# A down projection by seven products: other accumulators, another order of the products, and the operand sums moved behind one of them

## The chip, the cores and the metric

The kernel runs on one core of a Trainium2 chip. The core has five engines, each with its own queue of instructions: TensorE (PE in the profile; its weight loads are PEld), VectorE (DVE), ScalarE (ACT), GpSimd (POOL) and SyncE (SP), which issues most of the transfers. The metric is the device time of one execution in microseconds. TensorE writes its products into PSUM, which the kernel uses as eight banks of 128 x 512 fp32; everything else lies in SBUF.

## The reference

Two token batches, one of 512 and one of 256 tokens with 1024 features each, run through the same trunk of two layers. A layer is a feed-forward half step, a token mixer, and another feed-forward half step, each on a normalised input and added to the stream x:

```
x = x + 0.5 * swiglu_ffn(rmsnorm(x), w1, w2)
x = x + mixer(rmsnorm(x))
x = x + 0.5 * swiglu_ffn(rmsnorm(x), w1, w2)

gate, up = split(x @ w1, 2)          # w1 is 1024 x 5632
swiglu   = (silu(gate) * up) @ w2    # w2 is 2816 x 1024
```

There are four feed-forward steps in all. The mixers (a gated linear recurrence in the first layer, windowed attention in the second) are not touched by the change.

## The kernel before

All 768 tokens are handled together, as two halves of 384 (three blocks of 128 tokens). Every fp32 operand of a product is split into a high part, rounded to fp32r, and a low part that holds the rest. ScalarE makes the high part (a cast, L199 for weights and L266 for activations), VectorE the low part by a subtraction (L200 and L267). A product is then three matmuls: high by high, high by low, low by high.

A feed-forward step has 22 hidden chunks of 128. The first two go through the plain product. The others are treated as 2 x 2 block products that need seven block products instead of eight (a Strassen-Winograd scheme). The names p1 to p7 are these products. The weight blocks are a11, a12, a21 and a22. The weight operands of the seven are a11 (p1), a12 (p2), sums that are formed in place as the products are staged (p3, p6, p5), a22 (p4) and, for p7, two small tiles s3 that a transfer with addition on the POOL queue fills (L141).

**Up projection** (`up_pair`, L431). A pair of calls makes four hidden tiles, for two chunks and two token halves, named b00, b01, b10 and b11. In one call the products come in the order p1, p7, p2, p5, p4, p6, p3, each of 12 matmuls with 384 columns (`product`, L416). The tile for the second half is the last: it needs p3, then an addition (L453), the silu on ScalarE (L454), a product (L455), and the split into high and low part (L266, L267).

**Operand sums** (`mix`, L348, called through `gather`, L512). Four hidden tiles give the left operands of the down projection: b00, b10 and b11 directly, and t1 to t4 as sums of them (L350, L351, L353, L354), each of which is split as well. `FACTOR` (L45) says which product uses which operand: p1 b00, p2 b10, p3 b11, p4 t4, p5 t1, p6 t2, p7 t3. A group holds two sets of tiles (`kp` 0 and 1), the two K halves of its products.

**Down projection** (`down_quad`, L458). After each two pairs comes a group of seven products; there are five groups in a step (g = 0 to 4), 20 in the kernel. A product has three token blocks with a PSUM bank each, and six matmuls of 512 columns per block (two K halves by three; L479), so a group has 126. Every product has its result added from PSUM to the stream x by VectorE (`add_x`, L501), with factor 0.5 or -0.5. Three products add to the banks of another (`chain`): p2 to those of p1, p4 to those of p5, p3 to those of p7. Such a product may begin a block only when VectorE has read that bank. x itself is kept in a changed basis during the five groups: at g = 0 (L464, L465) and after the last group (L494, L495) sums of its four quarters are taken.

**Order.** The source order gives the priority; the instruction order of each engine is fixed when the program is built, by a planner that works with its own estimates of durations. An instruction whose inputs the planner thinks ready can be issued ahead of earlier ones of the source.

**Weights.** `plan_ffn` (L378) lists what is to be loaded. `load_next` loads the raw blocks into four raw buffers (L151, and L185 for s3). `stage_next` runs the next step of the listed order, which splits one operand. `done` gives back the slots of a product that has been issued and lets `ahead` stage as much as fits eight slots. A down operand takes two slots, so four are staged at a time: when a group begins, the first four of the listed order. In the step of p1, a11 is replaced by a11 + a21 (L206) once it has been split, and in the step of p2 a12 by a12 + a11 (L210). p3 is the split of the a12 so made.

Of the kernel before, what the change touches and what calls it, by code (L numbers as in the profile page):

```python
# [35 lines left out]
HB = H // P  # L36
# [4 lines left out]
SLOTS = 21  # L41
RING = 1024
UP = ("p1", "p7", "p2", "p5", "p4", "p6", "p3")
DOWN = ("p1", "p2", "p5", "p4", "p7", "p6", "p3")
FACTOR = {"p1": "b00", "p2": "b10", "p3": "b11", "p4": "t4", "p5": "t1", "p6": "t2", "p7": "t3"}  # L45


class Trunk:
# [291 lines left out]
    def put(self, name, kp, src):  # L340
        t = self.ops[(name, kp)] = self.big([P, 2, 2, H], F32R)
        self.split(src, t[:, :, 0, :], t[:, :, 1, :])
# [5 lines left out]
    def mix(self, b11, b12, b21, b22, put):  # L348
        sub = self.nc.vector.tensor_sub
        sub(b22, b12, b22)  # L350
        sub(b12, b11, b12)  # L351
        put("t1", b12)
        sub(b11, b11, b22)  # L353
        sub(b21, b21, b11)  # L354
        put("t4", b21)
        put("t3", b22)
        put("t2", b11)

    def sums(self):
        for kp in range(2):  # L360
# [17 lines left out]
    def plan_ffn(self, tag, w1, w2):  # L378
        def up(i):
            gate, up = (w1[:, c * P : (c + 1) * P] for c in (i, NF + i))  # L380
            if i < PLAIN:
                self.plan((tag, i, 0), gate, (NC, P))
                self.plan((tag, i, 1), up, (NC, P))
            else:
                self.plan_quad((tag, i), (gate, up), (NC, P), UP)

        for g in range(GROUPS):
            for i in range(4 * g, 4 * g + 4):
                up(i)
            rows = w2[4 * g * P : (4 * g + 4) * P, :].rearrange("(a k p) c -> k p a c", p=P, k=2)  # L390
            srcs = [rows[k][:, :, c * 512 : (c + 1) * 512] for c in range(2) for k in range(2)]
            self.plan_quad((tag, "down", g), srcs, (2, 512), DOWN)
        for i in range(NF - 2, NF):
            up(i)
        for c in range(2):
            self.plan((tag, "last", c), w2[(NF - 2) * P :, c * 512 : (c + 1) * 512], (2, 512))
# [58 lines left out]
        self.last_dve = nc.vector.tensor_mul(w, v, w).ins  # L455
        yield w

    def down_quad(self, tag, g, hid):  # L458
        nc = self.nc
        cols = lambda b, c: self.x[b][:, c * 512 : (c + 1) * 512]  # L460
        if g == 0:
            for i in range(HB):
                x12, x21, x22 = cols(HB + i, 0), cols(i, 1), cols(HB + i, 1)
                nc.vector.tensor_add(x12, x12, x22)  # L464
                nc.vector.tensor_sub(x21, x21, x22)  # L465
        banks = {}
        for name in DOWN:
            wh, wl = self.take((tag, "down", g, name))
            chain = {"p2": "p1", "p4": "p5", "p3": "p7"}.get(name, name)
            for i in range(HB):  # L470
                if name == chain:
                    banks[(chain, i)] = self.ps()
                ps = banks[(chain, i)]
                sl = slice(i * P, (i + 1) * P)
                for kp in range(2):
                    h = hid[FACTOR[name]]
                    a, w = (h[:, kp, 0, sl], h[:, kp, 1, sl]), (wh[:, kp, :], wl[:, kp, :])
                    for q, (x, y) in enumerate(((0, 0), (0, 1), (1, 0))):
                        nc.tensor.matmul(  # L479
                            ps,  # L480
                            a[x],
                            w[y],
                            start=name == chain and kp == 0 and q == 0,
                            stop=kp == 1 and q == 2,
                            skip_group_check=True,
                        )
                x22 = cols(HB + i, 1)
                dst = {"p2": cols(i, 0), "p4": cols(i, 1), "p3": cols(HB + i, 0)}.get(name, x22)
                self.add_x(dst, ps, -0.5 if name in ("p1", "p5") else 0.5)
            self.done((tag, "down", g, name))  # L490
        if g == GROUPS - 1:
            for i in range(HB):
                x12, x21, x22 = cols(HB + i, 0), cols(i, 1), cols(HB + i, 1)
                nc.vector.tensor_sub(x12, x12, x22)  # L494
                nc.vector.tensor_add(x21, x21, x22)  # L495

    def add_x(self, x, ps, c):
# [5 lines left out]
    def ffn(self, tag, next_row):  # L503
        for g in range(GROUPS):
            hid = {}

            def put(name, src, kp):
                if name not in hid:
                    hid[name] = self.big([P, 2, 2, H], F32R)
                self.split(src, hid[name][:, kp, 0, :], hid[name][:, kp, 1, :])  # L510

            def gather(ts, kp):  # L512
                self.mix(ts[0], ts[1], ts[2], ts[3], lambda name, src: put(name, src, kp))

            if g == 0:
                ts = {}
                for half in range(2):
                    for j in range(PLAIN):
                        t = ts[2 * j + half] = self.up_plain(tag, j, half)
                        name = f"b{j}{half}"  # L520
                        if name != "b01":
                            put(name, t, 0)
                gather(ts, 0)
                self.run_later(len(self.deferred))
            for kp in range(2):
                if g == 0 and kp == 0:
                    continue
                ts = []
                for j in range(2):
                    for half, t in enumerate(self.up_pair(tag, 4 * g + 2 * kp + j)):  # L530
                        ts.append(t)
                        name = f"b{j}{half}"
                        if name != "b01":
                            put(name, t, kp)
                gather(ts, kp)
            self.down_quad(tag, g, hid)
        hids = []
        for j in range(NF - 2, NF):
            hid = self.big([P, 2, T], F32R)
            for half, t in enumerate(self.up_pair(tag, j)):  # L540
                self.split(t, *(hid[:, i, half * H : (half + 1) * H] for i in range(2)))
            hids.append(hid)
        if next_row is None:
            self.load_final()
        banks = {}

        def add(b, k, hid):
            sl = slice(b * P, (b + 1) * P)
            for c in range(2):
                wh, wl = self.take((tag, "last", c))  # L550
                if k == 0:
                    banks[(b, c)] = self.ps()
                w = wh[:, k, :], wl[:, k, :]
                self.mm3(banks[(b, c)], (hid[:, 0, sl], hid[:, 1, sl]), w, k == 0, k == 1)
                if b == NBLK - 1 and k:
                    self.done((tag, "last", c))

        for b in range(NBLK):
            for i, k in (((0, 0), (1, 0), (0, 1)), ((1, 1),))[b] if b < 2 else ((b, 0), (b, 1)):
                add(i, k, hids[k])  # L560
            for c in range(2):
                self.add_x(self.x[b][:, c * 512 : (c + 1) * 512], banks[(b, c)], 0.5)
            self.after_block(b, next_row)
            if b >= 4:
                self.run_later()
# [716 lines left out]
```

## Time and profile before

| what | value |
| --- | --- |
| three runs, median (lowest to highest) | 2849.59 us (2848.89 to 2852.01) |
| the profiled execution, its own time | 2852.12 us |
| its span, first to last instruction | 2850.3 us |
| granted TensorE clock | 0.998 |
| matmuls of the up products (L421) | 6720, busy 1172.8 us |
| matmuls of the down products (L479) | 2520, busy 586.8 us |
| evictions to x (L501) | 468, busy 305.5 us |

The page lists the instructions of a kind with their busy time, the mean duration of one, and the idle time of their engine just before them, with what ended it. A matmul's recorded duration is longer than the distance from its start to the next one's start, because they overlap; so stretches on TensorE are better measured from start to start. The timeline merges neighbouring instructions of one line into a row: start, length, engine, line, operation, the count behind an x, and in brackets the idle time before it. Rows of stretches give the length, then for each engine its busy time and count.

### The profile page before, as it was taken

Reading aid. Unit: us, or ns where it says so; the run is one execution under the profiler, and the core shown is the slowest. Engines: PE = TensorE matmul, PEld = TensorE weight load, DVE = VectorE, ACT = ScalarE, POOL = GpSimd, SP = SyncE. Lnnn points to the kernel's source line nnn. Section 1 sums busy time; section 2 is a strip of 40 time slices with the busy share of each in tenths; the row PEclk is TensorE's granted clock in tenths of the full one; section 3 lists DMA queues with packets and bytes.
Section 4 is the critical chain, followed back from the end, with each engine's and each line's share of the span. In section 5 each row is a group of like instructions: output and inputs, shape, how many; then the busy total and the mean of one; then the engine's idle time right before and its main releaser. Section 6 shows DMA issues by size and latency. Waiting matters only on the chain. (4 is left out here: it accounts for less than half of the span.)

```text
span 2850.3 us, 40558 instructions
## 1 busy us (share of the span) xinstructions
PE 2796.7 (98%) x15225; PEld 2554.2 (90%) x15225; DVE 2173.2 (76%) x3750; ACT 1318.9 (46%) x2454; POOL 355.1 (12%) x402
## 2 busy tenths in 40 slices
PE   8999999999999999999999999999999899999998
PEld 8899999889899889998998998999888789989997
DVE  7788787468577658878878887887848878788877
ACT  7344443434344336434444643444458755434443
POOL 1111111000000001111111111111002211111110
PEclk9999999999999999999999999999999999999999
DMA  6554454311111133555444355545422113555443
GB/s 165 127 125 122 116 134 121 115 44 39 44 39 38 60 97 86 132 127 122 123 119 114 84 134 127 122 121 124 126 71 75 37 51 90 135 126 125 117 121 96
DMA packets 330101, 291.37 MB, mean 102 GB/s; under 512 B 11608, under 2 KB 257840, under 8 KB 329904
## 3 DMA queue, kind: packets, MB, share of 16 engines
q1 hardware_dynamic: 294064, 212.43, 25.4%
q0 software_dynamic: 31680, 62.93, 12.6%
q10 hardware_dynamic: 4160, 13.42, 1.3%
q8 instruction: 119, 1.95, 0.3%
q14 instruction: 78, 0.64, 0.1%
HBM read 216.39 MB, written 9.44 MB: 79 GB/s over the span
## 5 line engine op out<-in xcount | busy, mean ns | idle before, releaser
L421 PE MATMUL ps<-big,w 128*128 128x384 f32 x6720 | 1172.8, 334 | 3.1 <-DVE tA L444 2.9
L421 PEld LDWEIGHTS ps<-big,w 128*128 128x128 f32 x6720 | 1165.4, 188 | 8.8 <-DVE tA L444 7.2
L199 ACT CAST w<-wr 128x512 fp32r<-128x512 f32 x600 | 416.1, 707 | 722.7 <-PE ps L421 321.0
L479 PE MATMUL ps<-w,big 128*128 128x512 f32 x2520 | 586.8, 391 | 17.4 <-DVE x L501 17.4
L479 PEld LDWEIGHTS ps<-w,big 128*128 128x128 f32 x2520 | 469.4, 188 | 129.7 <-DVE x L501 17.3
L200 DVE TENSOR_TENSOR w<-wr,w 128x512 fp32r<-128x512 f32 (+1 forms) x520 | 438.1, 853 | 95.7 <-ACT w L199 87.0
L501 DVE SCALAR_TENSOR_TENSOR x<-ps,x 128x512 f32<-128x512 f32 x468 | 305.5, 682 | 20.5 <-PE ps L479 10.2
L141 POOL DMA_DIRECT2D s<-wr x120 | 105.4, 878 | 1333.4 <-DMA wr<-in_ffn_w_dram 583.0
L261 PE MATMUL ps<-w,big 128*128 128x512 f32 x624 | 249.8, 400 | 0.2
L263 PE MATMUL ps<-w,big 128*128 128x512 f32 x624 | 245.2, 393 | 2.5 <-DVE big L330 1.3
L262 PE MATMUL ps<-w,big 128*128 128x512 f32 x624 | 244.4, 392 | 0.0
L266 ACT CAST big<-tA 128x384 fp32r<-128x384 f32 x296 | 148.0, 513 | 175.0 <-DVE tA L449 72.0
L261 PE MATMUL ps<-big,w 128*128 128x384 f32 (+2 forms) x640 | 220.8, 346 | 3.3 <-ACT big L266 2.0
L262 PE MATMUL ps<-big,w 128*128 128x384 f32 (+2 forms) x640 | 216.8, 339 | 0.7 <-DVE big L267 0.5
L263 PE MATMUL ps<-big,w 128*128 128x384 f32 (+2 forms) x640 | 215.7, 337 | 0.0
L167 DVE TENSOR_TENSOR w<-wr,w 128x1024 fp32r<-128x1024 f32 x92 | 111.6, 1222 | 83.6 <-ACT w L166 59.7
L141 POOL DMA_DIRECT2D wr<-wr x100 | 87.5, 875 | 680.0 <-DVE tA L350 319.8
L267 DVE TENSOR_TENSOR big<-tA,big 128x384 fp32r<-128x384 f32 x296 | 164.2, 566 | 7.9 <-ACT big L266 4.4
L206 DVE TENSOR_TENSOR wr<-wr,wr 128x512 f32<-128x512 f32 (+1 forms) x100 | 79.3, 793 | 114.5 <-DMA wr<-wr 85.9
L166 ACT CAST w<-wr 128x1024 fp32r<-128x1024 f32 x92 | 96.6, 1052 | 120.5 <-PE ps L262 99.7
L263 PEld LDWEIGHTS ps<-w,big 128*128 128x128 f32 x624 | 117.4, 188 | 28.8 <-DVE big L330 2.0
L261 PEld LDWEIGHTS ps<-w,big 128*128 128x128 f32 x624 | 117.8, 189 | 22.3 <-issue 0.6
(170 smaller groups left out, 3317.2 us busy)
## 6 DMA issues: line engine op xcount, KB each, us to landing
wr<-in_ffn_w_dram SPq DMA_DIRECT2D x264, 512.0 KB, 3.9
s<-in_ffn_w_dram SPq DMA_DIRECT2D x120, 256.0 KB, 3.0
s<-wr POOLq DMA_DIRECT2D x120, 256.0 KB, 4.0
wr<-wr POOLq DMA_DIRECT2D x80, 256.0 KB, 4.0
wr<-in_hg_w_in_dram SPq DMA_DIRECT2D x40, 512.0 KB, 3.8
wr<-wr POOLq DMA_DIRECT2D x20, 512.0 KB, 4.6
spill<-x ACTq DMA_DIRECT2D x12, 512.0 KB, 3.0
x<-spill ACTq DMA_DIRECT2D x12, 512.0 KB, 3.3
```

The costliest lines, as they stand in the source:

```text
L141: self.nc.gpsimd.dma_start(out, src, accum_op=ALU.add)
L167: self.nc.vector.tensor_sub(lo, raw, hi.bitcast(F32))
L199: nc.scalar.copy(h, src)
L200: (eng or nc.vector).tensor_sub(l, src, h.bitcast(F32))
L261: nc.tensor.matmul(out, a[0], b[0], start=first, stop=False)
L262: nc.tensor.matmul(out, a[0], b[1], start=False, stop=False)
L263: nc.tensor.matmul(out, a[1], b[0], start=False, stop=last)
L266: self.nc.scalar.copy(hi, src)
L267: self.nc.vector.tensor_sub(lo, src, hi.bitcast(F32))
L421: self.nc.tensor.matmul(ps, a[x], b[y], start=first and k == 0 and i == 0, stop=k == 3 and i == 2, skip_group_check=True,)
L479: nc.tensor.matmul(ps, a[x], w[y], start=name == chain and kp == 0 and q == 0, stop=kp == 1 and q == 2, skip_group_check=True,)
L501: self.nc.vector.scalar_tensor_tensor(x, ps, c, x, ALU.mult, ALU.add)
```

## The change

The list `DOWN` says in which order the products are issued; a second list, `DOWN_STAGED`, says in which order their weights are staged (before, one list served both). The accumulators change: p2 still adds to p1's banks and p4 to p5's, p7 now adds to p3's. The results go to other quarters of x with other signs, and the basis at the first and after the last group is changed to fit. The number of matmuls and evictions stays.

The operand sums of the second set (`gather(ts, 1)`) are no longer formed before the group begins in the source, but inside it, ahead of p2, that is behind p1, p3 and their evictions. Within `mix` each sum is split as soon as it exists: t3, t1, t2, t4.

```diff
-DOWN = ("p1", "p2", "p5", "p4", "p7", "p6", "p3")
+DOWN = ("p1", "p3", "p2", "p7", "p5", "p6", "p4")
+DOWN_STAGED = ("p1", "p2", "p3", "p7", "p5", "p6", "p4")
...
         sub(b22, b12, b22)
         sub(b12, b11, b12)
+        put("t3", b22)
         put("t1", b12)
         sub(b11, b11, b22)
+        put("t2", b11)
         sub(b21, b21, b11)
         put("t4", b21)
-        put("t3", b22)
-        put("t2", b11)
...
-            self.plan_quad((tag, "down", g), srcs, (2, 512), DOWN)
+            self.plan_quad((tag, "down", g), srcs, (2, 512), DOWN_STAGED)
...
-    def down_quad(self, tag, g, hid):
+    def down_quad(self, tag, g, hid, gather):
...
                 x12, x21, x22 = cols(HB + i, 0), cols(i, 1), cols(HB + i, 1)
-                nc.vector.tensor_add(x12, x12, x22)
                 nc.vector.tensor_sub(x21, x21, x22)
+                nc.vector.tensor_add(x22, x22, x12)
         banks = {}
         for name in DOWN:
+            if name == "p2":
+                gather()
             wh, wl = self.take((tag, "down", g, name))
-            chain = {"p2": "p1", "p4": "p5", "p3": "p7"}.get(name, name)
+            chain = {"p2": "p1", "p4": "p5", "p7": "p3"}.get(name, name)
...
-                x22 = cols(HB + i, 1)
-                dst = {"p2": cols(i, 0), "p4": cols(i, 1), "p3": cols(HB + i, 0)}.get(name, x22)
-                self.add_x(dst, ps, -0.5 if name in ("p1", "p5") else 0.5)
+                dst = {"p2": cols(i, 0), "p4": cols(i, 1), "p7": cols(HB + i, 1)}.get(name, cols(HB + i, 0))
+                self.add_x(dst, ps, -0.5 if name == "p6" else 0.5)
...
-                nc.vector.tensor_sub(x12, x12, x22)
+                nc.vector.tensor_sub(x22, x22, x12)
                 nc.vector.tensor_add(x21, x21, x22)
...
-                gather(ts, kp)
-            self.down_quad(tag, g, hid)
+                if kp == 0:
+                    gather(ts, kp)
+            self.down_quad(tag, g, hid, lambda: gather(ts, 1))
```

## The prediction

> **What bounds the kernel now.** I read the page's busy line first, then its costliest groups, then the list of waits of TensorE.
>
> ```profile
> PE 2796.7 (98%) x15225; PEld 2554.2 (90%) x15225; DVE 2173.2 (76%) x3750; ACT 1318.9 (46%) x2454; POOL 355.1 (12%) x402
> ...
> L479 PE MATMUL ps<-w,big 128*128 128x512 f32 x2520 | 586.8, 391 | 17.4 <-DVE x L501 17.4
> ```
>
> ```profile
> PE ps L479 <- DVE x L501: 17.4, 37, 0.5
> ...
> PE ps L421 <- DVE tA L444: 2.9, 5, 1.1
> ```
>
> TensorE is busy for 98% of the span, so a microsecond counts only where TensorE stands still. Its largest wait in total is the down projection (L479) waiting for the evictions (L501): 37 waits, close to two for each of the 20 groups. The 17.4 us are counted from modelled matmul ends and are too small, so next I took the 20 stretches from a group's first matmul to the next product (five of them and the sum are shown), and the timeline of TensorE in two of them.
>
> ```profile
> core 0: us, PE busy (x) PEld busy (x) DVE busy (x) ACT busy (x) POOL busy (x), PEclk, DMA share, GB/s
> ...
> 262.81:293.01 30.20, 29.25 (x128) 23.49 (x127) 29.57 (x49) 10.01 (x18) 4.78 (x5) 1.00 0.55 137
> ...
> 1135.12:1164.91 29.79, 29.18 (x127) 23.49 (x127) 29.38 (x48) 10.02 (x18) 4.75 (x5) 1.00 0.56 138
> ...
> 1634.66:1664.07 29.41, 28.97 (x127) 23.51 (x127) 28.86 (x47) 10.02 (x18) 4.78 (x5) 1.00 0.56 140
> ...
> 1988.78:2018.39 29.61, 29.16 (x127) 23.47 (x127) 29.35 (x48) 10.01 (x18) 4.81 (x5) 1.00 0.56 136
> 2411.83:2441.41 29.58, 29.14 (x127) 23.48 (x127) 29.16 (x47) 10.01 (x18) 4.77 (x5) 1.00 0.56 139
> ...
> sum 600.95, PE 583.55 PEld 469.73 DVE 591.54 ACT 200.24 POOL 95.51; mean PE 29.18 PEld 23.49 DVE 29.58 ACT 10.01 POOL 4.78
> ```
>
> ```profile
> 262.81 4.28 PE L479 MATMUL ps<-w,big 128*128 128x512 f32 x18
> 267.63 10.29 PE L479 MATMUL ps<-w,big 128*128 128x512 f32 x44 [0.54 <-DVE x L501]
> 278.33 14.84 PE L479 MATMUL ps<-w,big 128*128 128x512 f32 x64 [0.41 <-DVE x L501]
> ```
>
> ```profile
> 1634.66 14.29 PE L479 MATMUL ps<-w,big 128*128 128x512 f32 x62
> ```
>
> The last row is a stretch without a wait: 62 matmuls, the last 0.39 us long, so one every (14.29 - 0.39) / 61 = 0.228 us. A group of 126 would take 28.7 us, 20 groups 574.2; they take 600.95. **26.7 us** are lost. In the regular group at 262.81 two waits carry it. The first stands behind 18 matmuls, which is p1: p2 should start at 262.81 + 18 x 0.228 = 266.91 and starts at 267.63, 0.72 late. The second stands behind 18 + 44 = 62 matmuls, eight more than p1, p2 and p5 have: eight matmuls of a later product were put ahead of p4 when the order was fixed at build, and still p4, due at 277.66, starts at 278.33, 0.67 late. All groups have the second wait (also the one without the first): 20 x 0.67 = 13.4 us. The first costs the rest, 13.3.
>
> Both have one cause: a product adds to the banks of the product just before it, and VectorE, which must read them in between, is late. Its rows around p1, and ScalarE's:
>
> ```profile
> 257.74 1.23 DVE L206 TENSOR_TENSOR wr<-wr,wr 128x1024 f32<-128x1024 f32 x1 [5.97 <-DMA wr<-wr]
> ...
> 260.02 0.55 DVE L444 TENSOR_TENSOR tA<-tA,ps 128x384 f32<-128x384 f32 x1
> 260.48 1.22 DVE L210 TENSOR_TENSOR wr<-wr,wr 128x1024 f32<-128x1024 f32 x1
> 261.62 1.22 DVE L200 TENSOR_TENSOR w<-wr,w 128x1024 fp32r<-128x1024 f32 x1
> 262.75 0.55 DVE L447 TENSOR_TENSOR tA<-tA,ps 128x384 f32<-128x384 f32 x1
> 263.33 0.56 DVE L448 TENSOR_TENSOR tA<-ps,tA 128x384 f32<-128x384 f32 x1
> ...
> 266.34 0.55 DVE L453 TENSOR_TENSOR tA<-tA,ps 128x384 f32<-128x384 f32 x1
> 266.80 0.68 DVE L501 SCALAR_TENSOR_TENSOR x<-ps,x 128x512 f32<-128x512 f32 x1
> 267.47 0.56 DVE L455 TENSOR_TENSOR tA<-tA,tA 128x384 f32<-128x384 f32 x1
> ...
> 268.61 0.56 DVE L267 TENSOR_TENSOR big<-tA,big 128x384 fp32r<-128x384 f32 x1
> 269.08 0.68 DVE L501 SCALAR_TENSOR_TENSOR x<-ps,x 128x512 f32<-128x512 f32 x1
> ...
> 274.66 1.88 DVE L501 SCALAR_TENSOR_TENSOR x<-ps,x 128x512 f32<-128x512 f32 x3
> ```
>
> ```profile
> 260.55 1.05 ACT L199 CAST w<-wr 128x1024 fp32r<-128x1024 f32 x1 [1.81 <-PE ps L421]
> ...
> 266.92 0.52 ACT L454 ACTIVATE tA<-tA 128x384 f32<-128x384 f32 x1 [1.55 <-DVE tA L453]
> 268.06 0.51 ACT L266 CAST big<-tA 128x384 fp32r<-128x384 f32 x1 [0.62 <-DVE tA L455]
> ```
>
> p1's first eviction runs 266.80 to 267.48; p2 starts 0.15 behind its end. That 0.15 is my price for a hand-over to TensorE.
>
> **The change part by part.** (1) Order and accumulators. Matmuls (126) and evictions (21) per group stay the same in number and size, so TensorE's floor of 28.7 us and VectorE's load stay. What moves is distance: p2 on p1's banks, p7 on p3's and p4 on p5's each get a whole product between, 18 x 0.228 = 4.1 us. p4's eviction was 0.67 late beyond eight matmuls (1.8 us) put ahead, 2.5 in all: 4.1 covers it, **minus 13.4 us**. p2's was 0.72 late and is covered as well. p7 needs p3's first eviction 4.1 + 12 x 0.228 = 6.8 us behind that block's end. Today's worst lag is p2's: its first block ends near 267.63 + 6 x 0.228 + 0.15 = 269.15 and its eviction near 274.66 + 0.68 = 275.34, 6.2 later, behind the operand sums. So no wait even with that lag, with 0.6 to spare; and the sums now come behind p3's evictions in the source.
>
> (2) What is late next: **p3's own operand**. p3 moves from last to second and multiplies b11, the group's youngest hidden tile. Its second K half needs b11's high part three matmuls into p3: 262.81 + 21 x 0.228 = 267.60. The chain L453, L454, L455, cast L266 ends at 268.06 + 0.51 = 268.57, with the hand-over 268.72: 1.12 late. The low part is needed two matmuls on, 269.18, and comes at 268.61 + 0.56 + 0.15 = 269.32: 0.14 more. Together 1.26 us in a regular group. In the four groups shown that have 29.79, 29.41, 29.61 and 29.58 us VectorE is ahead by what they lack to 30.20; the same comes off: 0.85, 0.47, 0.67, 0.64. Uncovered in all: 16 x 1.26 + 2.6 = 22.8 us, against the 26.7 lost today.
>
> How much is covered depends on the order fixed at build. The first halves of p3's second and third block need only old tiles: six matmuls, 1.37 us, that can stand ahead; this is what was done before p4. There the builder allowed 1.8 us for a lag of 2.5, and before p2 it allowed nothing for 0.72: its clock runs about 0.7 ahead of VectorE's. By that it sees 1.12 - 0.7 = 0.4 us at p3 and puts two matmuls (0.46) ahead. 0.66 remains, the low part is covered; with up to 0.27 from (3) I take the middle, 0.8. Ends: 0 (six ahead) and 1.53 (none ahead, all of (3)).
>
> [...]
>
> (3) Staging p1, p2, p3, p7. The third split in line (VectorE row 261.62) becomes p3's, whose source L210 writes; its cast (1.05) can start only at 260.48 + 1.22 = 261.70 and its subtraction at 262.8, while VectorE is free at 261.62. L447 and L448, each 0.47 start to start, can fill 0.94 of it: 0.27 of idle; a third operation fills all. With one it is 0.7, with none 1.2. The fourth split, p7's, is two halves of 512; their start-to-start of 0.6 makes 1.2 for 1.14 before: nothing. The sums p7 reads are queued on POOL ahead of the one that L206 already waited for at 257.74, so they are there.
>
> (4) Operand sums behind p3's evictions. Same eight VectorE and four ScalarE instructions. First used is t3, by p7's second half, three products and three matmuls after the start, 275.8 plus the new wait; today all eight are through by 274.66. TensorE's cover is p3 and p2; nothing. If the cover were gone, each operation late costs 0.47.
>
> (5) Banks and loads. p1 and p3 hold six of eight banks; the last bank of the pair is read by L453 until 266.89, before p3 starts at 266.91. The raw buffers come free in another order, so SP's next loads move:
>
> ```profile
> 262.86 3.49 SPq L151 DMA_DIRECT2D wr<-in_ffn_w_dram  x2
> ...
> 277.73 3.26 SPq L151 DMA_DIRECT2D wr<-in_ffn_w_dram  x2
> ```
>
> ```profile
> 282.60 0.62 ACT L199 CAST w<-wr 128x512 fp32r<-128x512 f32 x1 [5.62 <-PE ps L479]
> ...
> wr<-in_ffn_w_dram SPq DMA_DIRECT2D x264, 512.0 KB, 3.9
> ...
> wr<-wr POOLq DMA_DIRECT2D x80, 256.0 KB, 4.0
> ```
>
> The second of the first pair now waits for p5's split, behind p1: near 271 instead of 266. Landing 3.9 and POOL's sum 4.0 on top give 279, before the first cast of the next pair at 282.60. No cost. The six x updates of each first and last group keep their number and size: nothing.
>
> Sum: today 26.7; then 16 x 0.8 for the regular groups and about 1 for the other four, 13.8. Gain 12.9 us. The profiled execution took 2852.12 us (span 2850.3): it would be 2839.2. On the median of 2849.59, 0.09% lower, **2837 us**.
>
> **The rivals.** A, the forecast: p3's wait takes the place of p2's in part: 2837 (2831 to 2842).
>
> B: nothing is put ahead and p3 waits in full: 22.8 to 26.8 (with 0.2 of idle each), gain 0 to 4: 2846 to 2850. For it: nothing was put ahead of p2. Against: what stood ready there came from other products; here p3's own blocks do.
>
> C: p3's wait wholly covered by six matmuls: 2849.6 - 26.7 = 2823. For it: eight were put ahead before p4.
>
> D, the other side: p3's weight subtraction is issued with one operation or none between it and L210, VectorE stands 0.7 to 1.2 us for the cast, and b11 is that much later: 22.8 + 14 to 24 = 37 to 47 lost, 10 to 20 more than now: 2860 to 2870. It decides from (26.7 - 22.8) / 20 = 0.2 us of idle on, if nothing is put ahead. For it: L206 held L444 like this at 257.74. Against: L447 and L448 are ready. [...]
>
> E: the change removes TensorE's waits but VectorE, busy 29.58 of 30.05 us in a mean group, becomes the bound: gain 20 x 0.47 = 9.4, 2840. Against: 29.58 holds staging that is not due until the next pair.
>
> **How the numbers follow.** A 0.42, B 0.26, C 0.12, D 0.12, E 0.08. A measurement of this kernel can tell about 0.2%, 5.7 us. Faster by more: A's 0.40, C's 0.12, E's 0.06 and 0.05 of B, 0.63. Slower: 0.11 of D. The rest, 0.26, is same. Range 2823 to 2850: A, B, E and the upper half of C; D and the rest of C stay out, under 0.2.
>
> **What would show it.** Right: no wait before p2 and p4, one wait of 0.4 to 1.0 us in p3 three to nine matmuls in, a mean group near 29.4 us. Wrong: a wait three matmuls into p3 of over 1.1 us (B); VectorE idle before an L200 ahead of L449 (D); p7 waiting for L501 or t3; the stretches of L421 longer than now.

## The result and the profile after

The changed kernel takes 2876.22 us (median of five runs, 2871.48 to 2877.89); the kernel before took 2850.39 in the five runs beside it (2848.89 to 2852.01). The ratio is 1.0086 (95% interval 1.0075 to 1.0098): **slower by 0.86%**, where 2837 was forecast, and above the range's upper end of 2850. The profiled execution took 2871.75 us, with a span of 2870.0 and a granted clock of 0.995.

In the changed kernel the lines stand a little lower in the file: VectorE's weight subtraction is now L201 (L200 before) and its cast L200 (L199), the two sums in place are L207 and L211 (L206, L210), the tail of the up pair is L454 to L456 (L453 to L455), the split of an activation L267 on ScalarE and L268 on VectorE (L266, L267), the down matmuls L482 (L479), the evictions L503 (L501).

First the page's busy line and two of its costliest groups (busy us, mean ns, then the idle time of the engine just before them and what ended it), then TensorE's wait from the list of waits (us in total, times, longest):

```profile
PE 2801.7 (98%) x15225; PEld 2560.5 (89%) x15225; DVE 2179.1 (76%) x3750; ACT 1316.7 (46%) x2454; POOL 364.0 (13%) x402
...
L482 PE MATMUL ps<-w,big 128*128 128x512 f32 x2520 | 590.5, 394 | 34.0 <-ACT big L267 34.0
...
L201 DVE TENSOR_TENSOR w<-wr,w 128x512 fp32r<-128x512 f32 (+1 forms) x520 | 448.6, 870 | 121.0 <-ACT w L200 111.2
```

```profile
PE ps L482 <- ACT big L267: 34.0, 20, 2.2
```

The waits for evictions (37 of up to 0.5 us) are gone from the down matmuls. In their place stands one wait in each of the 20 groups, for the cast of an activation, up to 2.2 us long. It is one wait instead of two, and it is the longer.

The 20 stretches from a group's first matmul to the next product show the size (columns as before; four of the twenty and the sum):

```profile
core 0: us, PE busy (x) PEld busy (x) DVE busy (x) ACT busy (x) POOL busy (x), PEclk, DMA share, GB/s
84.53:115.78 31.25, 29.06 (x128) 23.50 (x128) 31.07 (x49) 10.93 (x20) 4.78 (x5) 1.00 0.54 131
...
263.33:295.74 32.41, 30.64 (x127) 24.63 (x127) 30.94 (x49) 10.52 (x19) 4.78 (x5) 0.95 0.52 123
354.45:385.15 30.70, 29.02 (x127) 23.50 (x127) 30.67 (x49) 10.42 (x19) 4.79 (x5) 1.00 0.53 129
...
1321.33:1354.17 32.84, 30.65 (x127) 24.63 (x127) 30.46 (x49) 10.93 (x20) 4.80 (x5) 0.95 0.54 130
...
sum 621.24, PE 587.24 PEld 474.52 DVE 613.16 ACT 208.88 POOL 95.67; mean PE 29.36 PEld 23.73 DVE 30.66 ACT 10.44 POOL 4.78
```

621.24 us against 600.95: 20.29 more, while the span grew by 19.7. So the whole loss lies in these stretches, and the rest of the kernel is 0.6 shorter. Against the prediction's floor of 574.2 the groups now lose 47.0 us. The clock column divides that: 16 groups have 1.00, four have 0.95. Those four keep TensorE busy for 30.6 us where the others have 29.0, 1.62 more for the same 126 matmuls: 6.5 us in all. The other 40.5 are the waits, 2.03 us a group.

Where the wait stands shows in the timeline of TensorE in two neighbouring groups, one with each clock:

```profile
263.33 4.96 PE L482 MATMUL ps<-w,big 128*128 128x512 f32 x21
270.06 25.84 PE L482 MATMUL ps<-w,big 128*128 128x512 f32 x105 [1.77 <-ACT big L267]
```

```profile
354.45 4.96 PE L482 MATMUL ps<-w,big 128*128 128x512 f32 x21
361.09 24.23 PE L482 MATMUL ps<-w,big 128*128 128x512 f32 x105 [1.68 <-ACT big L267]
```

Both stand after 21 matmuls: p1's 18 and three of p3. The next should start at 263.33 + 21 x 0.228 = 268.12 and starts at 270.06, 1.94 late. It is so in all 20 groups; in none was another matmul put ahead, and in none is there a second wait. VectorE's rows around p1, then ScalarE's:

```profile
257.82 1.23 DVE L207 TENSOR_TENSOR wr<-wr,wr 128x1024 f32<-128x1024 f32 x1 [5.15 <-DMA wr<-wr]
...
260.56 1.22 DVE L211 TENSOR_TENSOR wr<-wr,wr 128x1024 f32<-128x1024 f32 x1
262.97 1.23 DVE L201 TENSOR_TENSOR w<-wr,w 128x1024 fp32r<-128x1024 f32 x1 [1.19 <-ACT w L200]
264.11 0.55 DVE L448 TENSOR_TENSOR tA<-tA,ps 128x384 f32<-128x384 f32 x1
264.69 0.56 DVE L449 TENSOR_TENSOR tA<-ps,tA 128x384 f32<-128x384 f32 x1
...
266.10 1.29 DVE L201 TENSOR_TENSOR w<-s,w 128x512 fp32r<-128x512 f32 x2
267.30 0.55 DVE L268 TENSOR_TENSOR big<-tA,big 128x384 fp32r<-128x384 f32 x1
267.77 0.55 DVE L454 TENSOR_TENSOR tA<-tA,ps 128x384 f32<-128x384 f32 x1
...
268.91 0.56 DVE L456 TENSOR_TENSOR tA<-tA,tA 128x384 f32<-128x384 f32 x1
```

```profile
261.89 1.05 ACT L200 CAST w<-wr 128x1024 fp32r<-128x1024 f32 x1 [6.21 <-DVE wr L211]
...
269.50 0.51 ACT L267 CAST big<-tA 128x384 fp32r<-128x384 f32 x1 [0.62 <-DVE tA L456]
```

Read the bracket at 262.97 first. p3's weight subtraction stands directly behind L211, which writes its source. ScalarE's cast of that source starts at 261.89, 0.11 us after L211's end at 261.78, and takes 1.05; VectorE stands **1.19 us** for it, with L448 (264.11) and L449 (264.69) behind it. What L448 reads was there in time: the last matmul of p6, whose bank it takes, starts at 261.07 and ends at 261.40 by its record, before L211 ends. The same idle of 1.19 to 1.20 us is there in all 20 groups. From L207 to L454 it took 266.34 - 257.74 = 8.60 us before; now it takes 267.77 - 257.82 = 9.95, 1.35 more. L207 itself runs 5.51 us ahead of the group's first matmul instead of 5.07; it starts with the landing of a transfer. So the forecast's 1.12 us becomes 1.12 + 1.35 - 0.44 = 2.03, and with a hand-over of 0.05 (270.01 to 270.06) instead of 0.15, 1.93: the 1.94 that stand there. Behind each wait two more matmuls follow at 0.34 us instead of 0.228, which adds 0.2 to what the wait costs its group.

### The profile page after: what moved, and what is told of

Same layout as the page of the kernel before. It is cut to its first block, busy times and chain, and to the rows that moved or that the text cites. A ratio compares the mean times of both kernels' runs of the same rounds, so it can differ in the third digit from the quotient of the medians.

```text
span 2870.0 us, 40561 instructions
## 1 busy us (share of the span) xinstructions
PE 2801.7 (98%) x15225; PEld 2560.5 (89%) x15225; DVE 2179.1 (76%) x3750; ACT 1316.7 (46%) x2454; POOL 364.0 (13%) x402
## 5 line engine op out<-in xcount | busy, mean ns | idle before, releaser
L200 ACT CAST w<-wr 128x512 fp32r<-128x512 f32 x600 | 416.4, 706 | 768.9 <-PE ps L422 304.2
L482 PE MATMUL ps<-w,big 128*128 128x512 f32 x2520 | 590.5, 394 | 34.0 <-ACT big L267 34.0
L482 PEld LDWEIGHTS ps<-w,big 128*128 128x128 f32 x2520 | 474.2, 190 | 145.2 <-ACT big L267 42.4
L201 DVE TENSOR_TENSOR w<-wr,w 128x512 fp32r<-128x512 f32 (+1 forms) x520 | 448.6, 870 | 121.0 <-ACT w L200 111.2
L503 DVE SCALAR_TENSOR_TENSOR x<-ps,x 128x512 f32<-128x512 f32 x468 | 307.4, 683 | 16.9 <-PE ps L264 8.5
L267 ACT CAST big<-tA 128x384 fp32r<-128x384 f32 x296 | 150.8, 512 | 149.1 <-DVE tA L450 55.7
L268 DVE TENSOR_TENSOR big<-tA,big 128x384 fp32r<-128x384 f32 x296 | 163.3, 557 | 10.7 <-ACT big L267 10.4
L207 DVE TENSOR_TENSOR wr<-wr,wr 128x512 f32<-128x512 f32 (+1 forms) x100 | 80.5, 805 | 103.3 <-DMA wr<-wr 77.7
L201 POOL TENSOR_TENSOR w<-wr,w 128x512 fp32r<-128x512 f32 x80 | 130.7, 1634 | 154.3 <-ACT w L200 141.7
L264 PEld LDWEIGHTS ps<-w,big 128*128 128x128 f32 x624 | 117.4, 188 | 28.8 <-DVE big L331 2.0
```

The lines of the kernel that those rows point to most:

```text
L200: nc.scalar.copy(h, src)
L201: (eng or nc.vector).tensor_sub(l, src, h.bitcast(F32))
L264: nc.tensor.matmul(out, a[1], b[0], start=False, stop=last)
L267: self.nc.scalar.copy(hi, src)
L268: self.nc.vector.tensor_sub(lo, src, hi.bitcast(F32))
L482: nc.tensor.matmul(ps, a[x], w[y], start=name == chain and kp == 0 and q == 0, stop=kp == 1 and q == 2, skip_group_check=True,)
```

## The experiments

Theory 1 was: p3's weight subtraction, staged third, holds VectorE for the cast; this makes b11 late, and the long waits then lower the clock. The rivals were: the order as such, with p3 second and its operand the youngest, loses the time (2); the operand sums moved into the group do (3); the lower clock has a cause of its own, not the wait (4); and the accumulators themselves cost time, which the edit with another order (e2) is for. All edits are to the changed kernel, and ratios are to the kernel before in the same session.

### One place later in the staging order (e1_p3_staged_fourth)

```diff
-DOWN_STAGED = ("p1", "p2", "p3", "p7", "p5", "p6", "p4")
+DOWN_STAGED = ("p1", "p2", "p7", "p3", "p5", "p6", "p4")
```

> The changed kernel with p7's weights staged third and p3's fourth; nothing else. Theory 1 (VectorE stands 1.2 us for p3's weight cast, and the hidden tile b11 is late by that much more): VectorE's idle ahead of p3's weight subtraction goes, the wait three matmuls into p3 falls from 2.0 to about 1.1 us, groups with a half clock become none, 20 groups take about 597 us, the time is about 2850 (2845 to 2856). Theory 2 (p3's operand is late because p3 comes second, whatever is staged): the wait stays at 1.8 to 2.4 and the time within 0.2% of 2876.

2841.62 us, ratio 0.9965 (0.9952 to 0.9977). That is 3.4 us below the range of theory 1, for the wait left is smaller than the 1.1 us expected. VectorE's timeline at the same place, TensorE's in the group at 261.47, then the list of waits and the sum of the 20 stretches:

```profile
258.72 1.22 DVE L211 TENSOR_TENSOR wr<-wr,wr 128x1024 f32<-128x1024 f32 x1
259.86 1.29 DVE L201 TENSOR_TENSOR w<-s,w 128x512 fp32r<-128x512 f32 x2
261.06 0.55 DVE L448 TENSOR_TENSOR tA<-tA,ps 128x384 f32<-128x384 f32 x1
```

```profile
261.47 4.96 PE L482 MATMUL ps<-w,big 128*128 128x512 f32 x21
266.94 24.23 PE L482 MATMUL ps<-w,big 128*128 128x512 f32 x105 [0.51 <-ACT big L267]
```

```profile
PE ps L482 <- ACT big L267: 11.1, 18, 0.9
```

```profile
sum 592.01, PE 580.77 PEld 470.20 DVE 588.74 ACT 196.54 POOL 95.67; mean PE 29.04 PEld 23.51 DVE 29.44 ACT 9.83 POOL 4.78
```

Now p7's two half subtractions stand behind L211, and none of these rows carries an idle bracket; the idle of 1.19 us is gone from all 20 groups. The order of the products is the same, and one exchanged entry gives back 621.24 - 592.01 = 29.2 us: 22.7 of waits and the 6.5 of the slow clock, which is at 1.00 in all 20 groups. What stays is (592.01 - 574.2) / 20 = 0.89 us of wait a group, at the same place, three matmuls into p3 (in two of the groups it is too short to show in the list). So rival 2, the order as such, explains 17.8 us of the 47.0. That is less than the 26.7 that were lost before the change.

### The sums ahead of the group again (e4_sums_before_group)

```diff
         banks = {}
+        gather()
         for name in DOWN:
-            if name == "p2":
-                gather()
```

> The changed kernel with all operand sums formed ahead of the group in the source, as before the change; order and staging stay the changed ones. Theory 1 (the operand sums lie behind b11's chain either way): p3's wait stays at 1.8 to 2.4 us and the time within 0.3% of 2876 (2867 to 2885). Theory 2 (the moved sums push b11's chain back): the wait falls by 0.9 us, time about 2855.

2876.68 us, ratio 1.009 (1.0075 to 1.0105): the changed kernel's own time.

```profile
sum 627.28, PE 591.90 PEld 478.19 DVE 610.40 ACT 211.17 POOL 96.80; mean PE 29.59 PEld 23.91 DVE 30.52 ACT 10.56 POOL 4.84
```

The idle of 1.19 us and the wait three matmuls into p3 are there in every group. The groups sum to 6.0 us more than the changed kernel's; seven of them are at 0.95 instead of four, which is 3 x 1.62 = 4.9 of it. Rival 3 falls: moving the sums costs nothing and brings nothing. The order in which `mix` splits the sums stays the changed one here, so it was not undone by itself.

### p3 with its old K half first (e6_p3_by_k_halves)

The loops of p3 are turned: first the K half whose operands are old for all three blocks, then the other. All else, the staging too, stays.

```diff
-            for i in range(HB):
+            steps = [(i, kp) for i in range(HB) for kp in range(2)]
+            if name == "p3":
+                steps = [(i, kp) for kp in range(2) for i in range(HB)]
+            for i, kp in steps:
...
```

> The changed kernel with p3's loops turned: the first K half of its three blocks, then the second, so b11's second half is wanted nine matmuls into p3 and not three, 1.37 us later; the same matmuls in all. Theory 1 (only b11's arrival limits p3): the wait falls from 2.0 to 0.6 to 0.7 us, now nine matmuls into p3, no group at a half clock, 20 groups about 588 us, time 2838 (2833 to 2845). Theory 2 (a clock or VectorE bound of the whole group): the time stays over 2860.

2836.23 us, ratio 0.9951 (0.9936 to 0.9966). TensorE's timeline of the group at 261.51:

```profile
261.51 6.32 PE L484 MATMUL ps<-w,big 128*128 128x512 f32 x27
268.49 22.87 PE L484 MATMUL ps<-w,big 128*128 128x512 f32 x99 [0.66 <-ACT big L267]
```

```profile
sum 587.82, PE 580.57 PEld 470.21 DVE 586.86 ACT 208.20 POOL 95.76; mean PE 29.03 PEld 23.51 DVE 29.34 ACT 10.41 POOL 4.79
```

27 matmuls instead of 21 stand ahead of the wait. Six matmuls cover 6 x 0.228 = 1.37 us: 2.03 - 1.37 = 0.66 should be left, 20 x 0.66 + 574.2 = 587.4, and 587.82 is measured. VectorE's idle of 1.2 us is still there. Putting these matmuls ahead is what I had counted on the builder (the planner that fixes the order) to do by itself, at least in part.

### The wait filled with matmuls (e5_idle_filled)

Nine matmuls more in each group, behind p1, into a bank that nobody reads: 2.05 us, about the length of the wait.

```diff
+            if name == "p1":
+                spare = self.ps()
+                for r in range(9):
+                    nc.tensor.matmul(spare, hid["b00"][:, 0, 0, :P], wh[:, 0, :], start=True, stop=True)
             self.done((tag, "down", g, name))
```

> The changed kernel with nine extra matmuls of 128x512 behind p1 in every group, into a spare bank that nobody reads: 9 x 0.228 = 2.05 us of work where TensorE waits 1.5 to 2.4 us. Theory 1 (a wait of about 2 us makes the granted clock fall in some groups, and that costs 1.6 us a group on top): the wait left at p3 is 0 to 0.4 us, no group shows a clock under 1.00, the longest group is near 31.3 us instead of 32.8, the sum of the 20 groups is 612 to 622 and the lowest and highest time lie closer together; time 2863 to 2873. Theory 2 (the half clock has another cause, the chip or the load of VectorE and the transfers): some groups still show 0.95 and the time is 2876 or more, as much longer as the extra matmuls outlast the wait.

2871.0 us (2868.75 to 2872.33), ratio 1.0068 (1.0053 to 1.0083). One of the stretches and the sum:

```profile
175.52:206.77 31.25, 31.07 (x136) 25.20 (x136) 30.65 (x49) 11.21 (x20) 4.79 (x5) 1.00 0.58 135
...
sum 618.54, PE 617.73 PEld 505.14 DVE 612.84 ACT 216.31 POOL 96.92; mean PE 30.89 PEld 25.26 DVE 30.64 ACT 10.82 POOL 4.85
```

All 20 groups are at 1.00. With 180 matmuls more the groups are 2.7 us shorter than the changed kernel's. The ratios' intervals overlap, so the times alone don't prove a gain; the clock column does show that the slow clock goes with the standing still, and not with the place or the work around it. The granted clock of whole executions agrees: it is 0.993 to 0.996 in the nine of the changed kernel and of e4, which have the full wait, and 0.997 to 0.999 in all others on record, those of the kernel before and of the other six edits. Rival 4 falls.

### The accumulators with another order (e2_order_alone)

p2 directly behind p1 as before the change, p3 fifth, p7 last, one list for both orders, the sums ahead of the group. What stays of the change is the accumulators, the order in which `mix` splits the sums, and the distance between p5 and p4, p3 and p7.

```diff
-DOWN = ("p1", "p3", "p2", "p7", "p5", "p6", "p4")
-DOWN_STAGED = ("p1", "p2", "p3", "p7", "p5", "p6", "p4")
+DOWN = ("p1", "p2", "p5", "p6", "p3", "p4", "p7")
+DOWN_STAGED = DOWN
```

> The changed kernel's accumulators, but products in the order p1, p2, p5, p6, p3, p4, p7 (staged alike) and all operand sums ahead of the group in the source: p3 late again, p4 and p7 each with one product or more between them and their bank's owner, p2 right behind p1. Theory 1 (the distance to p4 is worth 13.4 us, p3's place costs all the rest): p2 waits 0.7 us as before the change, no second wait, 20 groups about 588 us, time 2837 (2833 to 2842), faster than both. Theory 2 (the accumulators themselves, or x updates in another basis, cost): time over 2850.

2839.63 us, ratio 0.996 (0.9946 to 0.9975), groups 588.97. The time came out near what I expected, for another reason in part. Neither p4 nor p7 waits for an eviction, as expected. p2's wait is only 0 to 0.7 us, 5.5 in all; and a new one of about 0.4 us stands in every group, five matmuls into p5, where the low part of t1's second half is not ready. So the gain from the distance is real (p4's 13.4 us are gone), the accumulators cost nothing that shows, and an operand sum is the next to be late.

### Both mends together (e7_both_mends), and p3 around p2 (e3_p3_around_p2)

The first joins e1's staging with e6's loops. The second cuts p3 in two, its old K half ahead of p2 and its young one behind, and moves p3 to the fourth place of the staging and t1 ahead of t3:

```diff
-DOWN = ("p1", "p3", "p2", "p7", "p5", "p6", "p4")
-DOWN_STAGED = ("p1", "p2", "p3", "p7", "p5", "p6", "p4")
+DOWN = ("p1", "p3a", "p2", "p3b", "p5", "p7", "p6", "p4")
+DOWN_STAGED = ("p1", "p2", "p5", "p3", "p7", "p6", "p4")
...
-        put("t3", b22)
         put("t1", b12)
+        put("t3", b22)
```

> The changed kernel with p7 staged third and p3 fourth, and p3's loops turned to K halves. Theory 1 (the two shifts of b11 and of its use add up: the wait of 0.2 to 1.1 us left by the staging alone is under the 1.37 us gained by turning the loops): no wait in p3, 20 groups about 574 us, time about 2824 (2820 to 2829). Theory 2 (VectorE, busy nearly all of a group, becomes the bound): groups stay near 29.4 us, time 2835 to 2842.

> The changed accumulators with p3's first K half ahead of p2 and its second half behind p2, then p5, p7, p6, p4; staged p1, p2, p5, p3, p7, p6, p4; sums split in the order t1, t3, t2, t4. b11's second half is wanted 6.2 us behind p1's end instead of 0.7, p2's banks have nine matmuls (2.05 us) in between. Theory 1: no wait in the group, 20 groups about 574 us, time 2824 (2819 to 2829), faster than every other version or level with the turned loops. Theory 2 (VectorE is the bound of a group): 2835 to 2842.

e7: 2819.67 us, ratio 0.9891 (0.9874 to 0.9907). e3: 2817.03 us, ratio 0.9881 (0.9866 to 0.9895). Both came out faster than the ranges given, e7 by 0.3 and e3 by 2.0 us. The sum of the 20 stretches of e7, then one group of e3 in TensorE's timeline:

```profile
sum 572.11, PE 572.11 PEld 473.28 DVE 571.75 ACT 196.86 POOL 95.70; mean PE 28.61 PEld 23.66 DVE 28.59 ACT 9.84 POOL 4.78
```

```profile
258.74 28.76 PE L483 MATMUL ps<-w,big 128*128 128x512 f32 x126
```

126 matmuls in one row: no wait is left in the groups. The two parts of the loss add up as theory 1 has it. With the idle gone (e1) b11 is up to 1.1 us late, and six matmuls cover 1.37. **Both versions beat both kernels**, by 1.1 and 1.2% against the kernel before. A group stands at 28.60 us; my floor of 28.7 was 0.1 too high, so the losses counted against it are 0.1 a group too small. e3's span of 2815.6 is 34.7 shorter than before, of which 28.9 lie in the groups; the other 5.8 are spread over the rest, and their cause was not followed.

## Why the prediction was wrong

**The forecast's sum failed in step (3), staging.** The sum had 13.8 us of loss, 0.8 for a regular group, and in that at most 0.27 for staging, because "L447 and L448, each 0.47 start to start, can fill 0.94 of it". Neither was put there. VectorE stands idle for 1.19 us in all 20 groups, the value I had named for "none", and b11 is that much later. With that entry of the staging exchanged (e1) 22.7 us of waits go, and with them 6.5 us of slow clock. I used two operations as filler because they were ready in time; being ready was not enough: L448's input was there at 261.40, and VectorE's rows show both at 264.11 and 264.69, behind the subtraction that waited until 262.97.

This was rival D, with its place and nearly its time (the profiled execution's 2871.75 is 2 us beyond 2860 to 2870, the median 6). Its price, 37 to 47 us lost, holds the 40.5 of waits. That the whole 47.0 stands at its upper end is luck: D took 22.8 for the wait without the idle, where e1 leaves 17.8, and had nothing for the clock's 6.5. A chance of 0.12 was much too low: my own trace of before had a case, L444 held by L206. Why the builder chose this place stays open; its estimates can't be read from a trace.

**(1) Order and accumulators: right.** p4's and p2's waits are gone and p7 waits for nothing in the changed kernel. There the wait in p3 holds back the group's other 105 matmuls (the row at 270.06), and could hide such waits; e7 has the same order of products and no wait at all, so none is hidden.

**(2) p3's own operand: right place, wrong cover.** The wait stands where forecast, three matmuls into p3, for b11's high part. Without the idle it is smaller than worked out: e1 loses 0.89 us a group, where I had 22.8 / 20 = 1.14. In e1's group at 261.47 the matmul that waits is 0.68 late (266.94 instead of 266.26), where I had 1.12 for a regular group. From L207 to the end of b11's cast it takes 266.89 - 255.98 = 10.91 us there, against 268.57 - 257.74 = 10.83 before. But L207 runs 5.49 us ahead of the group's first matmul instead of 5.07, and the hand-over is 0.05: 1.12 + 0.08 - 0.42 - 0.10 = 0.68. The cover was wrong: the builder "puts two matmuls (0.46) ahead" does not hold in any of the 20 groups, in e1 neither. I had taken its eight matmuls before p4 as a rule; p2, ahead of which it had put nothing, was the better witness. Without D the result would have been about e1's 2841.6. That is rival B's mechanism, a little better than its 2846; that it lies inside the forecast's own 2831 to 2842 would have been luck.

**(4) and (5): right.** The moved sums change nothing (e4), and no load or bank is waited for: the wait in p3 is the only one of the groups.

**Rival E falls.** VectorE is busy for 28.59 of 28.61 us in e7's mean group, and TensorE doesn't wait, so that work was not due yet. In e2's mean group it is busy for 26.82 of 29.45.

**Not foreseen: the clock.** Four of the 20 groups of the profiled execution lose 1.62 us more at half clock behind the wait. That is 6.5 of the 47.0 us lost, and no term of the sum stood for it.

## What to carry to other kernels

When a product is moved forward, count how old its youngest operand is, and follow the chain that makes it through every engine on its way: here the waits of 0.72 and 0.67 us at p2 and p4 went, and one of 1.94 came at p3. In the changed kernel a subtraction that needed ScalarE's cast of what had just been written held VectorE for about the length of the cast (1.19 us of idle for a cast of 1.05); in e1, with p7's two half subtractions between, that idle was gone. Staging another operand first was worth 29.2 us here, more than the 26.7 that the groups of the kernel before lost. Where one K half of a product is old and the other young, issue all of the old half first (e6: 587.82 us in the groups instead of 621.24).

## What the runs showed of the hardware

Behind four of the 20 waits of about 2 us the granted clock of TensorE fell to 0.50 for 3.41 us; with the wait filled by matmuls (e5) all 20 groups are at 1.00. The rows give the granted clock (third column from the end) in the group at 263.33, whose wait ends at 270.06:

```profile
270.06:271.00 0.94, 0.94 (x4) 0.60 (x5) 0.94 (x3) 0.90 (x1) 0.37 (x1) 1.00 0.02 6
271.00:272.00 1.00, 1.00 (x5) 0.76 (x4) 1.00 (x2) 0.00 (x0) 0.49 (x1) 0.66 0.07 16
272.00:273.00 1.00, 1.00 (x4) 0.80 (x3) 0.94 (x2) 0.00 (x0) 0.00 (x0) 0.50 1.07 182
273.00:274.00 1.00, 1.00 (x4) 0.81 (x3) 0.49 (x1) 0.00 (x0) 0.00 (x0) 0.50 0.90 169
274.00:275.00 1.00, 1.00 (x4) 0.77 (x4) 0.66 (x2) 0.00 (x0) 0.00 (x0) 0.63 1.04 305
275.00:276.00 1.00, 1.00 (x6) 0.81 (x5) 0.47 (x1) 0.70 (x1) 0.00 (x0) 1.00 0.43 127
```

At half clock from 271.32 (0.66 is a third at full) to 274.74: 3.42 us. Worked out in the same way from stretches of 0.2 us, the half clock lasts 3.41 to 3.42 us in all four groups of the changed kernel and in all seven of e4, and within each execution the starts lie a whole number of 3.4133 us apart (in the changed kernel 271.32 to 1148.54 is 257.0 of them, 1148.54 to 1329.45 is 53.0, and again 53.0 to 1510.36: 1239.04 / 363 = 3.4133). In these 3.41 us eight matmuls start 0.427 us apart instead of 0.227: 8 x 0.2 = 1.6 us, the 1.62 lost.

The length of a wait alone does not tell which group gets the half clock: 1.66 us of standing still (from a matmul's recorded end to the next one's start) in the group at 1140.29 is followed by it, 2.19 us in the one at 84.53 is not. So I counted off periods of 3.4133 us from these starts, in both directions, and took how much of a wait falls into one period. The period before 271.32 began at 267.91 and holds the whole wait that ended at 270.06. In the 40 groups of the changed kernel and of e4, 11 have at least 1.74 us of standing still in one such period, and 10 of these are followed by half clock; of the 29 with less, one is (1.66). The bound of 1.74 was chosen after these figures were seen, and no run shows why the clock falls behind such a period. One of the longest waits of the changed kernel, in the group at 84.53, costs no clock:

```profile
91.69 24.25 PE L482 MATMUL ps<-w,big 128*128 128x512 f32 x105 [2.19 <-ACT big L267]
```

Its 2.19 us fall into two periods, 0.92 and 1.27. The one group with 1.86 us in a period that stayed at full clock was not explained.
